# One half bank for all three terms of a product, pairs of column tiles per bank, fewer convolution taps on GpSimd

## The chip, the cores and the metric

One core of a Trainium2 chip runs the whole layer. The metric is device time in microseconds (us) of one launch, lower is better. The engines are named as in the profile: PE is TensorE's matmul side, PEld its weight load, DVE is VectorE, ACT is ScalarE, POOL is GpSimd, SP is SyncE, which issues the transfers.

## The reference, cut to what matters

One layer on 256 tokens with 2048 channels (16 row tiles of 128), everything in float32:

```
h = RMSNorm(x);  u = h @ W_in                       # 34 column tiles of 128
A: 6 heads   y_A = B * conv3(C * v)                 # short heads, 3 tiles each
B: 6 heads   GLU -> causal conv of 31 taps -> LayerNorm -> swish   # 2 tiles each
C: 4 groups  trailing mean over 2, 4, 8, 16 frames minus self -> 128x128 product
x = x + RMSNorm(concat(y_A, y_B, y_C) @ W_out)      # 16 column tiles
h = RMSNorm(x);  [g, v] = conv3(h @ W_up)           # 88 column tiles
x = x + RMSNorm((silu(g) * v) @ W_down)             # 44 row tiles
```

The scale of RMSNorm is one number for each token, so the kernel multiplies by it after the product (`r_bc`: the scales spread over all partitions), not before.

## The kernel before, in words

**The stream.** The weights come as 364 units of half a megabyte, [128 x 1024] float32: 68 of w_in, 32 of w_out, 176 of w_up, 88 of w_down, numbered through, so w_out begins at unit 68 and w_up at unit 100. Each unit is split into two float32r parts: ACT copies it to `whi` (L101), DVE subtracts that from the raw unit and leaves `wlo` (L108). `ahead(i)` splits up to unit i + 4. Two units of w_up (`POOL_UNITS`, 105 and 107) are subtracted by POOL. A unit holds 8 blocks of 128x128, for 8 products.

**The product** (L231 to L245). Activations lie as (hi, lo) pairs, 2 x 256 columns. For one block and one row tile PE runs a 512-column matmul `w_hi @ [h_hi, h_lo]` (L243) and a 256-column one, `w_lo @ h_hi` (L233); a column tile has a bank of its own. The bank's halves are added up afterwards: `fold` (L273) copies the right half with ACT (L275) and adds it with DVE (L276). Only the last tile of w_out, o15, uses the form `folded`: three 256-column matmuls into one half (L236, L237, L233).

**The order.** The first 4 column tiles of w_in, w_out and w_up are computed together (`mm_group`, 2 row tiles for each unit, 8 units), since their operands come only little by little; all others one after the other (`mm_columns`, 2 units, 16 products). `IN_ORDER`: the conformer heads' pairs (value, gate), the 4 pools, then the short heads. After each column tile some steps of `background` are issued (`PACE`). Small products (pool, LayerNorm's mean) are issued by `later` a number of units after their operand. A scheduler that estimates times puts the unpinned instructions of every engine in an order at build time; at run time each engine works in that order and only waits.

**A conformer head.** `head_glu` folds value and gate, scales them, and multiplies them on POOL (`glu`). Of its 31 taps, DVE takes 15 as multiply-adds (`tap`, L372); for the other `POOL_TAPS` = 14 ACT makes the scaled copies (L391) and POOL adds them up (L392). After the sixth head LayerNorm follows: POOL adds the heads up (`lnt`, L419), PE sums that over the channels (`ln_mean`, L425), and so on.

**Second norm and gated MLP.** The scale of the first norm comes back as `bc_y`; DVE scales y (L615), adds x (L619) and makes h's low part (L299), ACT its high part, two row tiles for each unit of the first group of w_up. A gate pair j (`gate`) folds both its tiles, scales them by `r2_bc` (L690), makes the two three-tap convolutions (ACT L691, DVE L693), Silu (ACT L700), product (POOL L702) and the two parts (ACT L703, DVE L704). At j = 4 and some later pairs DVE also transposes a part of the residual (L671). Row tiles 0 and 1 of the group wait for `r2_bc`, which is made after the group.

Of the kernel before, what the change touches and what calls it, by code (L numbers as in the profile page):

```python
# [14 lines left out]
P = 128  # L15
T = 256
# [10 lines left out]
# Columns of the packed per-channel parameters.  # L27
# [6 lines left out]
for _name, _w in _FIELDS:  # L34
# [9 lines left out]
IN_ORDER = (  # L44
    [x for i in range(N_HEADS) for x in (18 + i, 24 + i)]
    + [30 + g for g in range(N_POOL)]
    + [x for i in range(N_HEADS) for x in (6 + i, 12 + i, i)]
)
# The order in which the row tiles of w_out are contracted.
# [13 lines left out]
def trunk_kernel(ctx: ExitStack, tc, xt, vec, g_row, pool_w, w_in, w_out, w_up, w_down, out):  # L63
# [39 lines left out]
    def split_lo(i, pieces=1):  # L103
        raw = raws.pop(i)
        hi, lo = parts[i]
        eng = nc.gpsimd if i in POOL_UNITS else nc.vector
        for s in cut(pieces):
            ins = eng.tensor_tensor(lo[:, s], raw[:, s], hi[:, s].bitcast(F32), ALU.subtract)  # L108
            if eng is nc.vector:
                pin(ins)  # L110
# [15 lines left out]

# [1 line left out]
    # `background` holds elementwise work in order; `late` holds small products that  # L128
    # are issued a few units after their operands were, so that TensorE needn't wait.
# [41 lines left out]
    # TensorE's clock rises while it works: it is kept busy until the first weights are in.  # L171
    # The first activation loads ScalarE's table in that time.
    idle = const.tile([P, 512], BF16, name="idle")
# [4 lines left out]
    def keep_busy(n):  # L178
        warm = psum.tile([P, 512], F32, tag="mm", name="warm")
        for _ in range(n):  # L180
            tc.keep_in_program_order(
                nc.tensor.matmul(warm, idle[:, :P], idle, start=True, stop=True)
            )
# [20 lines left out]
    def squares_by_token(parts_, name):  # L204
        """Tiles [channels, n * T] that add up to the squares -> [tokens, 2 halves], in PSUM."""
# [13 lines left out]
    def over_partitions(r, name):  # L219
        """[tokens, 2 halves] -> [all partitions, tokens], in PSUM."""  # L220
# [8 lines left out]
    # Activations are kept as [channels, k, (hi, lo), T]; a product leaves w_hi @ lo in the  # L229
    # second half of its bank, or adds it to the first where `folded` is set.  # L230
    def product(ps, w_hi, w_lo, h, first, last, folded=False):  # L231
        def by_lo():
            nc.tensor.matmul(ps[:, :T], w_lo, h[:, 0], start=False, stop=folded and last)  # L233

        if folded:
            nc.tensor.matmul(ps[:, :T], w_hi, h[:, 0], start=first, stop=False)  # L236
            nc.tensor.matmul(ps[:, :T], w_hi, h[:, 1], start=False, stop=False)  # L237
            by_lo()
            return
        if last:  # L240
            by_lo()
        both = h.rearrange("p j t -> p (j t)")
        nc.tensor.matmul(ps, w_hi, both, start=first, stop=last)  # L243
        if not last:
            by_lo()  # L245

    def mm_columns(u0, name, ht, order=NATURAL, folded=False):
        ps = psum.tile([P, 512], F32, tag="mm", name=name)
        for h in range(2):
            ahead(u0 + h)  # L250
            whi, wlo = parts.pop(u0 + h)
            for kk in range(8):
                k = 8 * h + kk
                c = slice(kk * P, (kk + 1) * P)
                product(ps, whi[:, c], wlo[:, c], ht[:, order[k]], k == 0, k == KD - 1, folded)
            tick()
        return ps

    def mm_group(u0, name, ht, before, order=NATURAL):
        pss = [psum.tile([P, 512], F32, tag="mm", name=f"{name}{m}") for m in range(GROUP)]  # L260
        for kg in range(8):
            before(kg)
            ahead(u0 + kg)
            whi, wlo = parts.pop(u0 + kg)
            for kk in range(2):
                k = 2 * kg + kk
                for m, ps in enumerate(pss):
                    c = slice((kk * GROUP + m) * P, (kk * GROUP + m + 1) * P)
                    product(ps, whi[:, c], wlo[:, c], ht[:, order[k]], k == 0, k == KD - 1)
            tick()  # L270
        return pss

    def fold(ps, right, out):  # L273
        """The two halves of a bank, added up; `right` is scratch."""
        nc.scalar.activation(right, ps[:, T:], AF.Copy)  # L275
        nc.vector.tensor_tensor(out, ps[:, :T], right, ALU.add)  # L276
        return out

    # ================= token mixing =================
    with tc.tile_pool(name="mix", bufs=1) as mix, tc.tile_pool(name="mixt", bufs=2) as mixt:  # L280
# [23 lines left out]
        def start(kg):  # L304
            for k in (2 * kg, 2 * kg + 1):
                make_hi(k, h1, "g_mix")
                make_lo(k, h1, "g_mix")
                if k == 0:
                    split_hi(0, 2)
                    split_lo(0, 2)  # L310
                    done[0] = 1
            if 0 < kg < 5:
                load_x(2 * kg + 6, 2)
            square_sum(two(xT, kg), sum_x, kg == 0, f"sqx{kg}")

        first = mm_group(0, "in", h1, start)
        got = dict(zip(IN_ORDER, first))

# [28 lines left out]
        def tmp(name):  # L347
            return mixt.tile([P, T], F32, tag="t", bufs=10, name=name)

        def folded(ps, name):  # L350
            return fold(ps, tmp(f"{name}r"), tmp(name))
# [494 lines left out]
```

## Time and profile before

| | us |
|---|---|
| median of 3 runs | 1096.47 (1096.30 to 1096.82) |
| span of the profiled execution | 1094.2 |
| PE busy | 1050.7 (96%) |
| DVE busy | 774.7 (71%) |
| ACT busy | 593.6 (54%) |
| POOL busy | 244.9 (22%) |
| granted TensorE clock, mean over the span | 0.993 |

The span runs from the first to the last instruction of one execution; the time of a run is some 2.3 us longer. Busy time is not time on the path: PE is at work nearly all the time, so what can be won or lost is the time in which PE waits or runs at a lower clock, and the number and length of its matmuls. The chain that ended last is mostly PE's own; where it leaves PE, it leaves it for what PE waited for. A start in the timeline and the next start of the same kind give the pitch, which is what a pipelined matmul costs; its printed length (its end is modelled) is longer than that.

### The profile page before, as it was taken

The numbers are of one execution on the slowest core, as the hardware profiler recorded it, in microseconds if no ns is written. First come the engines' busy times: TensorE is split into PE (matmuls) and PEld (weight loads), VectorE is DVE, ScalarE is ACT, GpSimd is POOL, SyncE is SP. The second block draws the span as 40 slices with busy tenths as digits, with TensorE's granted clock in tenths as the row PEclk, the third lists the DMA queues.
The fourth block names the chain that finished last, engine by engine and source line by source line (L and its number), as shares of the span: only waits on it lengthen the run. The fifth ranks groups of instructions, "written<-read, shape, count | busy, mean of one in ns | idle before, by whom it ended". The sixth has DMA issues, their size and how long they took to land.

```text
span 1094.2 us, 15331 instructions
## 1 busy us (share of the span) xinstructions
PE 1050.7 (96%) x5565; PEld 885.7 (81%) x5565; DVE 774.7 (71%) x1042; ACT 593.6 (54%) x920; POOL 244.9 (22%) x260
## 2 busy tenths in 40 slices
PE   8987989699998999999999999999999999999997
PEld 5876778588886888888888888888888888888885
DVE  7899986775549886877778788788787444444444
ACT  8674466565555655655556566555555343343432
POOL 4386479742224220101101010000000000000001
PEclk9999999899999999999999999999999999999999
DMA  7634554446553537666486676555556655565552
GB/s 270 214 128 142 177 173 147 158 158 208 183 186 113 174 122 244 187 169 226 138 246 190 175 234 207 179 190 189 185 183 228 192 182 188 191 191 183 187 189 77
DMA packets 73452, 199.78 MB, mean 183 GB/s; under 512 B 23712, under 2 KB 24480, under 8 KB 73248
## 3 DMA queue, kind: packets, MB, share of 16 engines
q1 hardware_dynamic: 73088, 197.72, 56.9%
q8 instruction: 44, 0.72, 0.3%
q10 hardware_dynamic: 288, 1.07, 0.2%
q14 instruction: 32, 0.26, 0.1%
HBM read 194.57 MB, written 2.10 MB: 180 GB/s over the span
## 4 chain that ended last, share of the span: by engine, by line
PE 82%; DVE 7%; POOL 6%; issue 3%; ACT 1%; DMA 0%; SPq 0%; DVEq 0%; POOLq 0%; ACTq 0%
PE gate L243 14%; PE val L243 14%; PE d L736 8%; PE d L737 8%; PE d L738 7%; PE gate L233 7%; PE val L233 7%; PE o L243 5%; PE in L243 4%; POOL accp L392 3%; PE o L233 3%; DVE acc L372 3%; PE in L233 2%; DVE wlo L108 2%; DVE h L299 1%
## 5 line engine op out<-in xcount | busy, mean ns | idle before, releaser
L108 DVE TENSOR_TENSOR wlo<-raw,whi 128x1024 fp32r<-128x1024 f32 (+1 forms) x363 | 465.3, 1286 | 225.7 <-ACT whi L101 223.1
L101 ACT ACTIVATE whi<-raw 128x1024 fp32r<-128x1024 f32 (+1 forms) x365 | 383.1, 1053 | 264.8 <-PE d L738 135.1
L243 PE MATMUL gate<-h,whi 128*128 128x512 f32 x672 | 241.1, 399 | 0.0
L243 PE MATMUL val<-h,whi 128*128 128x512 f32 x672 | 241.0, 399 | 0.0
L243 PE MATMUL in<-h,whi 128*128 128x512 f32 x544 | 193.2, 403 | 4.2 <-DVE h L299 2.7
L233 PE MATMUL gate<-h,wlo 128*128 128x256 f32 x672 | 182.1, 281 | 0.0
L233 PE MATMUL val<-h,wlo 128*128 128x256 f32 x672 | 182.0, 281 | 0.0
L233 PE MATMUL in<-h,wlo 128*128 128x256 f32 x544 | 149.1, 287 | 12.2 <-DVE wlo L108 12.2
L243 PEld LDWEIGHTS val<-h,whi 128*128 128x128 f32 x672 | 126.4, 188 | 27.1
L243 PEld LDWEIGHTS gate<-h,whi 128*128 128x128 f32 x672 | 126.4, 188 | 26.9
L702 POOL TENSOR_TENSOR cg<-cg,cv 128x256 f32<-128x256 f32 x44 | 49.2, 1118 | 426.1 <-DVE cv L693 386.9
L738 PE MATMUL d<-whi,g_lo 128*128 128x512 f32 x352 | 138.8, 394 | 0.0
L736 PE MATMUL d<-whi,g_hi 128*128 128x512 f32 x352 | 138.8, 394 | 0.0
L737 PE MATMUL d<-wlo,g_hi 128*128 128x512 f32 x352 | 138.8, 394 | 0.0
L233 PEld LDWEIGHTS gate<-h,wlo 128*128 128x128 f32 x672 | 127.0, 189 | 4.9 <-DVE wlo L108 0.7
L233 PEld LDWEIGHTS val<-h,wlo 128*128 128x128 f32 x672 | 127.0, 189 | 4.2
L243 PEld LDWEIGHTS in<-h,whi 128*128 128x128 f32 x544 | 101.7, 191 | 26.9 <-DVE h L299 3.6
L233 PEld LDWEIGHTS in<-h,wlo 128*128 128x128 f32 x544 | 103.1, 191 | 21.1 <-DVE wlo L108 18.5
L243 PE MATMUL o<-y_t,whi 128*128 128x512 f32 x240 | 83.7, 395 | 0.0
L736 PEld LDWEIGHTS d<-whi,g_hi 128*128 128x128 f32 x352 | 65.9, 187 | 16.4
L738 PEld LDWEIGHTS d<-whi,g_lo 128*128 128x128 f32 x352 | 65.9, 187 | 16.2
L737 PEld LDWEIGHTS d<-wlo,g_hi 128*128 128x128 f32 x352 | 65.9, 187 | 16.2
(232 smaller groups left out, 1066.3 us busy)
## 6 DMA issues: line engine op xcount, KB each, us to landing
raw<-in_w_up SPq DMA_DIRECT2D x176, 512.0 KB, 3.7
raw<-in_w_down SPq DMA_DIRECT2D x88, 512.0 KB, 3.5
raw<-in_w_in SPq DMA_DIRECT2D x67, 512.0 KB, 3.8
raw<-in_w_out SPq DMA_DIRECT2D x32, 512.0 KB, 3.5
xT<-blocks SPq DMA_DIRECT2D x64, 32.0 KB, 3.8
out<-tail_sb SPq DMA_DIRECT2D x8, 256.0 KB, 2.3
xT<-in_xt SPq DMA_DIRECT2D x7, 256.0 KB, 5.5
tail_sb<-in_g_row ACTq DMA_DIRECT2D x1, 1024.0 KB, 6.7
```

The lines of the kernel that those rows point to most:

```text
L101: pin(nc.scalar.activation(hi[:, s], raws[i][:, s], AF.Copy))
L108: ins = eng.tensor_tensor(lo[:, s], raw[:, s], hi[:, s].bitcast(F32), ALU.subtract)
L233: nc.tensor.matmul(ps[:, :T], w_lo, h[:, 0], start=False, stop=folded and last)
L243: nc.tensor.matmul(ps, w_hi, both, start=first, stop=last)
L299: pin(nc.vector.scalar_tensor_tensor(ht[:, k, 1], xT[:, k], v(gain, k), ht[:, k, 0].bitcast(F32), ALU.mult, ALU.subtract,))
L372: nc.vector.scalar_tensor_tensor(a[:, o:], glu[:, : T - o], cb(s), a[:, o:], ALU.mult, ALU.add)
L392: nc.gpsimd.tensor_tensor(ap[:, o:], ap[:, o:], p[:, : T - o], ALU.add)
L702: nc.gpsimd.tensor_tensor(a, a, b, ALU.mult)
L736: nc.tensor.matmul(pss[h], g_hi[:, k, s], w1, start=(k == 0), stop=False)
L737: nc.tensor.matmul(pss[h], g_hi[:, k, s], w2, start=False, stop=False)
L738: nc.tensor.matmul(pss[h], g_lo[:, k, s], w1, start=False, stop=(k == KF - 1))
```

## The change

`product` now always makes three 256-column matmuls into one half bank, w_hi with h_hi, w_hi with h_lo, w_lo with h_hi, so nothing is folded. Two column tiles share a bank, one in each half (`mm_column`, `mm_pair`), and are read out together where they belong together: one 512-wide DVE multiply by the scale for a conformer head (`vg`), a gate pair (`u`) or two short heads' B tiles (`br`); the squares and copies of w_out's tiles read PSUM on ACT without a fold. The scalings of the short heads' C and B tiles and of the heads' values, on POOL before, are on DVE now. `POOL_TAPS` is 8, so DVE takes 21 taps of a head and POOL adds 7 copies and the sum. `POOL_UNITS` is gone. The first group of w_out and of w_up holds 8 column tiles (one row tile for each unit, 16 units), that of w_in still 4. Short heads come two at a time (C and v, C and v, B and B). `tmp` has 7 buffers instead of 10. The background's steps are counted by kind of pair (`PACE`) and in w_out 4 for each unit until the tenth. In the second norm the steps are spread over units of one row tile.

```diff
-GROUP = 4
+GROUP_IN, GROUP_OUT, GROUP_UP = 4, 8, 8
-POOL_UNITS = (68 + 32 + 5, 68 + 32 + 7)
-POOL_TAPS = 14  # taps of a conformer head that GpSimd adds up
+POOL_TAPS = 8
-PACE = (5, 4, 4)
+PACE = {"head": 5, "pool": 4, "cv": 4, "b": 5}
...
+    def product(ps, w_hi, w_lo, h, first, last):
+        terms = ((w_hi, h[:, 0]), (w_hi, h[:, 1]), (w_lo, h[:, 0]))
+        for n, (w, x) in enumerate(terms):
+            nc.tensor.matmul(
+                ps, w, x, start=first and n == 0, stop=last and n == 2, skip_group_check=True
+            )
...
+    def mm_pair(u0, name, ht, order=NATURAL, between=None):
+        ps = bank(name)
+        mm_column(u0, ps[:, 0], ht, True, order)
+        if between:
+            between()
+        mm_column(u0 + 2, ps[:, 1], ht, False, order)
         return ps
...
-        def head_glu(i, val, gate):
-            sg = folded(gate, f"sg{i}")
-            nc.vector.tensor_tensor(sg, sg, stats["r"], ALU.mult)
-            nc.scalar.activation(sg, sg, AF.Sigmoid)
-            vr = folded(val, f"vr{i}")
-            nc.gpsimd.tensor_tensor(vr, vr, stats["r"], ALU.mult)
+        def head_glu(i, ps):
+            vg = mixt.tile([P, 2, T], F32, tag="vg", name=f"vg{i}")
+            nc.vector.tensor_tensor(vg, ps, twice(stats["r"]), ALU.mult)
+            nc.scalar.activation(vg[:, 1], vg[:, 1], AF.Sigmoid)
             glu = glu6[:, i]
-            nc.gpsimd.tensor_tensor(glu, vr, sg, ALU.mult)
+            nc.gpsimd.tensor_tensor(glu, vg[:, 0], vg[:, 1], ALU.mult)
...
-        def gate(j, pg, pv):
-            a = conv3(pg, j, "cg")
+        def gate(j, ps):
+            u = ffnt.tile([P, 2, T], F32, tag="u", name=f"u{j}")
+            nc.vector.tensor_tensor(u, ps, twice(r2_bc), ALU.mult)
+            a = conv3(u[:, 0], j, "cg")
             nc.scalar.activation(a, a, AF.Silu)
-            b = conv3(pv, KF + j, "cv")
+            b = conv3(u[:, 1], KF + j, "cv")
...
-        for j in range(GROUP // 2, KF):
-            pg = mm_columns(u0, f"gate{j}", h2)
-            if j == GROUP // 2:
-                for i in range(j):
-                    gate(i, *first[2 * i : 2 * i + 2])
-            pv = mm_columns(u0 + 2, f"val{j}", h2)
+        n_first = GROUP_UP // 2
+        for j in range(n_first, KF):
+            ps = mm_pair(
+                u0, f"gv{j}", h2,
+                between=(lambda: [gate(i, first[i]) for i in range(n_first)])
+                if j == n_first else None,
+            )
             u0 += 4
-            gate(j, pg, pv)
+            gate(j, ps)
```

How this moves instructions is shown at two places. The first is DVE where the gated MLP has just begun. Before, the single tile gate5 (`gate_4012`) is folded and scaled between the transpose and the split of units 124 and 125 (`wlo_4016` and the next), before which PE still has val5's two units (122, 123) to do:

```order
L671 STREAM_TRANSPOSE blocks_4010<-xT 128x1024
L276 TENSOR_TENSOR u_4102<-gate_4012,cg_4103 128x256
L690 TENSOR_TENSOR u_4102<-u_4102,r_bc 128x256
L693 SCALAR_TENSOR_TENSOR cg_4103<-u_4102,vec_sb,cg_4103 128x255
L693 SCALAR_TENSOR_TENSOR cg_4103<-u_4102,vec_sb,cg_4103 128x254
L108 TENSOR_TENSOR wlo_4016<-raw_4013,whi_4015 128x1024
L108 TENSOR_TENSOR wlo_4038<-raw_4035,whi_4037 128x1024
```

Now the pair gv5 (`gv_4614`, units 120 to 123) stands there, and `wlo_4618` is unit 124, the first of the next pair; the split before it on DVE, unit 123's, lies 30 rows ahead:

```order
L710 TENSOR_TENSOR u_4735<-gv_4614,r_bc 128x512
L703 SCALAR_TENSOR_TENSOR cg_4737<-u_4735,vec_sb,cg_4737 128x255
L703 SCALAR_TENSOR_TENSOR cv_4742<-u_4735,vec_sb,cv_4742 128x255
L703 SCALAR_TENSOR_TENSOR cg_4737<-u_4735,vec_sb,cg_4737 128x254
L716 TENSOR_TENSOR g_lo<-cg_4600,g_hi 128x256
L684 STREAM_TRANSPOSE blocks_4612<-xT 128x1024
L703 SCALAR_TENSOR_TENSOR cv_4742<-u_4735,vec_sb,cv_4742 128x254
L114 TENSOR_TENSOR wlo_4618<-raw_4615,whi_4617 128x1024
```

What moved is the read of a finished tile: it now stands ahead of the split of the unit that PE takes right after that tile. On ACT at the same place the row of before is this, with the copy of the unit (`whi_4015`) one step behind gate5's convolution:

```order
L703 ACTIVATE g_hi<-cg_3991 128x256
L275 ACTIVATE cg_4103<-gate_4012 128x256
L691 ACTIVATE cg_4103<-u_4102,vec_sb 128x256
L101 ACTIVATE whi_4015<-raw_4013 128x1024
L101 ACTIVATE whi_4037<-raw_4035 128x1024
L700 ACTIVATE cg_4103<-cg_4103 128x256
```

Now both convolutions of gv5 and its Silu stand ahead of unit 124's copy (`whi_4617`):

```order
L701 ACTIVATE cg_4737<-u_4735,vec_sb 128x256
L701 ACTIVATE cv_4742<-u_4735,vec_sb 128x256
L715 ACTIVATE g_hi<-cg_4600 128x256
L712 ACTIVATE cg_4737<-cg_4737 128x256
L108 ACTIVATE whi_4617<-raw_4615 128x1024
```

Unit 124's copy has moved behind work that needs the last product of unit 123. The second place is POOL ahead of LayerNorm's mean, at the end of w_in before (the sum `lnt_994` is what `ln_mean` reads, and the short heads' scalings `br` and `cr` stand between):

```order
L392 TENSOR_TENSOR accp<-accp,p_30_1984 128x243
L521 TENSOR_TENSOR br_2099<-br_2099,r_bc 128x256
L395 TENSOR_TENSOR acc_408<-acc_408,accp 128x240
L523 TENSOR_TENSOR ya_2103<-br_2099,sa_2040 128x256
L377 TENSOR_TENSOR acc_408<-acc_408 128x255
L419 TENSOR_TENSOR lnt_994<-lnt_994,acc_408 128x256
L507 TENSOR_TENSOR cr_2164<-cr_2164,rr_bc 128x256
```

Now those scalings are gone from POOL, the sum is `lnt_1089`, and PE's `ln_mean` stands among the products of the w_out group, after the second of its 16 units:

```order
L399 TENSOR_TENSOR accp<-accp,p_30_2523 128x249
L402 TENSOR_TENSOR acc_470<-acc_470,accp 128x234
L384 TENSOR_TENSOR acc_470<-acc_470 128x255
L426 TENSOR_TENSOR lnt_1089<-lnt_1089,acc_470 128x256
L526 TENSOR_TENSOR br_2726<-br_2726,sa_2437 128x256
```

## Rows read from the trace of the kernel before

**Rows 1.** The page: span, and the chain that ended last by engine.

```profile
span 1094.2 us, 15331 instructions
...
PE 82%; DVE 7%; POOL 6%; issue 3%; ACT 1%; DMA 0%; SPq 0%; DVEq 0%; POOLq 0%; ACTq 0%
```

**Rows 2.** Waits of PE, 36 to 240 us: total us, times, longest.

```profile
PE in L233 <- DVE wlo L108: 11.9, 13, 2.2
PE ln_mean L425 <- POOL lnt L419: 7.5, 1, 7.5
PE pool L493 <- DVE pooled L486: 5.3, 4, 1.7
```

**Rows 3.** PE's timeline, start and length: first product after the group, first of w_out.

```profile
36.58 0.47 PE L243 MATMUL in<-h,whi 128*128 128x512 f32 x1
...
239.55 0.40 PE L243 MATMUL o<-y_t,whi 128*128 128x512 f32 x1
```

**Rows 4.** Windows: length, busy PE, PEld, DVE, ACT, POOL, PE clock, DMA, GB/s.

```profile
197.00:207.00 10.00, 5.19 (x26) 3.54 (x24) 8.72 (x11) 6.30 (x11) 9.53 (x11) 1.00 0.34 116
207.00:217.00 10.00, 5.08 (x19) 4.34 (x20) 7.21 (x11) 4.27 (x9) 6.22 (x8) 0.66 0.54 169
```

**Rows 5.** DVE's timeline in w_in: splits of units 16 and 43, taps, a quiet split.

```profile
53.06 1.22 DVE L108 TENSOR_TENSOR wlo<-raw,whi 128x1024 fp32r<-128x1024 f32 x1
...
74.77 3.43 DVE L372 SCALAR_TENSOR_TENSOR acc<-glu,vec_sb,acc 128x252 f32<-128x252 f32 x4
...
126.12 1.22 DVE L108 TENSOR_TENSOR wlo<-raw,whi 128x1024 fp32r<-128x1024 f32 x1
127.26 1.23 DVE L372 SCALAR_TENSOR_TENSOR acc<-glu,vec_sb,acc 128x250 f32<-128x250 f32 x3
...
144.83 1.22 DVE L108 TENSOR_TENSOR wlo<-raw,whi 128x1024 fp32r<-128x1024 f32 x1
```

**Rows 6.** POOL's timeline beside the first taps of rows 5.

```profile
77.02 8.12 POOL L392 TENSOR_TENSOR accp<-accp,p 128x251 f32<-128x251 f32 x8
```

**Rows 7.** PE's timeline: products of o14, of o15 (folded form), two tiles of w_up.

```profile
318.72 0.39 PE L243 MATMUL o<-y_t,whi 128*128 128x512 f32 x1
...
323.25 0.40 PE L243 MATMUL o<-y_t,whi 128*128 128x512 f32 x1
...
324.31 0.28 PE L236 MATMUL o<-y_t,whi 128*128 128x256 f32 x1
...
328.20 0.28 PE L236 MATMUL o<-y_t,whi 128*128 128x256 f32 x1
...
828.17 0.40 PE L243 MATMUL gate<-h,whi 128*128 128x512 f32 x1
...
833.82 0.40 PE L243 MATMUL val<-h,whi 128*128 128x512 f32 x1
```

**Rows 8.** Waits of PE over the whole span, the first group of w_up.

```profile
PE up L243 <- DVE h L299: 4.6, 4, 2.1
```

**Rows 9.** Timelines of DVE and POOL in that group.

```profile
349.00 4.03 DVE L299 SCALAR_TENSOR_TENSOR h<-xT,vec_sb,h 128x256 fp32r<-128x256 f32 x2
...
350.18 2.56 POOL L108 TENSOR_TENSOR wlo<-raw,whi 128x1024 fp32r<-128x1024 f32 x1
```

**Rows 10.** Timelines of DVE and ACT: durations used for the gate pairs.

```profile
335.73 0.68 DVE L615 TENSOR_TENSOR yo<-yo,bc_y 128x512 f32<-128x512 f32 x1
...
396.47 0.48 DVE L693 SCALAR_TENSOR_TENSOR cv<-u,vec_sb,cv 128x254 f32<-128x254 f32 x1
...
404.45 1.24 DVE L671 STREAM_TRANSPOSE blocks<-xT 128x1024 f32<-128x1024 f32 x1
...
406.55 0.60 ACT L691 ACTIVATE cg<-u,vec_sb 128x256 f32<-128x256 f32 x1 [1.67 <-DVE u L690]
407.06 1.99 ACT L101 ACTIVATE whi<-raw 128x1024 fp32r<-128x1024 f32 x2
408.95 0.40 ACT L700 ACTIVATE cg<-cg 128x256 f32<-128x256 f32 x1
```

More of the change, by code (lines that the diff above doesn't have):

```diff
@@ L227, in over_partitions, with bank, mm_column @@
         return ps[:, :T]
[L231 to L248, printed above, removed]
+    def product(ps, w_hi, w_lo, h, first, last):
+        terms = ((w_hi, h[:, 0]), (w_hi, h[:, 1]), (w_lo, h[:, 0]))
+        for n, (w, x) in enumerate(terms):
+            nc.tensor.matmul(
+                ps, w, x, start=first and n == 0, stop=last and n == 2, skip_group_check=True
+            )
+    def bank(name):
+        return psum.tile([P, 2, T], F32, tag="mm", name=name)
+    def mm_column(u0, ps, ht, opens, order=NATURAL):
         for h in range(2):
@@ L254, in mm_columns, with mm_group, twice @@
                 c = slice(kk * P, (kk + 1) * P)
-                product(ps, whi[:, c], wlo[:, c], ht[:, order[k]], k == 0, k == KD - 1, folded)
+                product(ps, whi[:, c], wlo[:, c], ht[:, order[k]], opens and k == 0, k == KD - 1)
             tick()
-        return ps
[L259 to L269, printed above, removed]
+    def mm_pair(u0, name, ht, order=NATURAL, between=None):
[4 more added lines that the diff above has]
+        mm_column(u0 + 2, ps[:, 1], ht, False, order)
+        return ps
+    def mm_group(u0, name, ht, n, before, order=NATURAL):
+        pss = [bank(f"{name}{m}") for m in range(n // 2)]
+        rows = 8 // n
+        for u in range(KD // rows):
+            for kk in range(rows):
+                before(rows * u + kk)
+            ahead(u0 + u)
+            whi, wlo = parts.pop(u0 + u)
+            for kk in range(rows):
+                k = rows * u + kk
+                for m in range(n):
+                    c = slice((kk * n + m) * P, (kk * n + m + 1) * P)
+                    product(
+                        pss[m // 2][:, m % 2], whi[:, c], wlo[:, c], ht[:, order[k]],
+                        k == 0 and m % 2 == 0, k == KD - 1,
+                    )
             tick()
         return pss
[L273 to L277, printed above, removed]
+    def twice(t):
+        return t[:, None, :].to_broadcast([P, 2, T])
     with tc.tile_pool(name="mix", bufs=1) as mix, tc.tile_pool(name="mixt", bufs=2) as mixt:
@@ L302, in make_lo, with start @@
             ))
[L304 to L317, printed above, removed]
+        def start(k):
+            make_hi(k, h1, "g_mix")
+            make_lo(k, h1, "g_mix")
+            if k == 0:
+                split_hi(0, 2)
+                split_lo(0, 2)
+                done[0] = 1
+            kg = k // 2
+            if k % 2:
+                if 0 < kg < 5:
+                    load_x(2 * kg + 6, 2)
+                square_sum(two(xT, kg), sum_x, kg == 0, f"sqx{kg}")
+        first = mm_group(0, "in", h1, GROUP_IN, start)
         edge = mix.tile([P, N_POOL, 16], F32, name="edge")
@@ new lines, in short_conv, with short_gate @@
+            nc.vector.tensor_tensor(cv, ps[:, 1], cv, ALU.mult)
+            a = tmp(f"sa{i}")
+            nc.scalar.activation(a, cv, AF.Copy, scale=ca(2))
+            for s in (1, 2):
+                nc.vector.scalar_tensor_tensor(
+                    a[:, s:], cv[:, : T - s], ca(2 - s), a[:, s:], ALU.mult, ALU.add
+                )
+            stats[f"a{i}"] = a
+        def short_gate(i, ps):
+            br = mixt.tile([P, 2, T], F32, tag="vg", name=f"br{i}")
+            nc.vector.tensor_tensor(br, ps, twice(stats["r"]), ALU.mult)
+            for j in range(2):
+                nc.gpsimd.tensor_tensor(br[:, j], br[:, j], stats.pop(f"a{i + j}"), ALU.mult)
+                keep(i + j, br[:, j])
@@ L552, in trunk_kernel, with scales_a, between @@
+        def scales_a():
+            stats["rx"] = token_rsqrt([sum_x], D, RMS_EPS, "x")
+        later(1, scales_a)
+        later(2, token_scales)
+        def between(kind):
             while waiting:
                 evacuate(*waiting.pop(0))
-            run_background(PACE[0 if 18 <= m < 30 else 1 if m >= 30 else 2])
-        sum_y = mix.tile([P, T], F32, name="sum_y")
+            run_background(PACE[kind])
+        for kind, i, _ in IN_PAIRS[GROUP_IN // 2 :]:
+            ps = mm_pair(u0, f"in_{kind}{i}", h1, between=lambda: between(kind))
+            u0 += 4
+            waiting.append((kind, i, ps))
+            between(kind)
@@ L810, in _lay_out, with by_columns @@
     ], axis=1))
-    def by_columns(w, order, rows=None):
+    def by_columns(w, order, group, rows=None):
         t = w.reshape(KD, P, -1, P)
```

207 lines of the change are left out of this document (94 added, 113 removed).

## The prediction, made before the changed kernel ran

> **What bounds the kernel now.** I read the page first: the chain that ended last is 82% PE, with 7% DVE and 6% POOL, in a span of 1094.2 us; a run takes 1096.47, so 2.3 us lie outside the span and I add them at the end [rows 1]. The kernel is bound by PE's matmuls; the 13% of DVE and POOL are places where PE waited for them. So I asked next for PE's waits, and then for PE's timeline stage by stage, against the time that the products alone would take.
>
> The pitch of a product, start to start, is (833.82 − 828.17)/16 = 353.1 ns over a whole w_up tile [rows 7]. In w_in, from the first product after the group to the first of w_out, there are 59 units of 8 products: 472 x 0.3531 = 166.7 us, with the small products (scales, pools, LayerNorm) perhaps 5 more. It took 239.55 − 36.58 = 203.0 us [rows 3]. So **31 us are lost in w_in**: 11.9 in 13 waits for DVE's `wlo`, 5.3 in 4 waits of the pool products for DVE's `pooled`, 7.5 in one wait of `ln_mean` for POOL's `lnt` [rows 2]. The other 6 or so are slow matmuls: after the long wait the granted clock is 0.66 of 2.4 GHz in the mean of 207 to 217, part of the 10 us at the lower level, 1.2 GHz, worth up to 3.4 us [rows 4]; the rest lies around the shorter waits. The other place is the first group of w_up, with 4.6 us in 4 waits for h's low part [rows 8]. Everywhere else PE streams, and there only the product itself counts.
>
> **Why DVE is late in w_in.** Between the splits of units 16 and 43 it took 144.83 − 53.06 = 91.8 us, while PE needs 27 x 8 x 0.3531 = 76.3 [rows 5]. A tap costs (1.23 − 0.48)/2 = 0.38 quiet, start to start (three in 1.23, one alone being 0.48 long), and 3.43/4 = 0.86 or a little less while POOL adds [rows 5, 6, 10]. POOL's eight adds took 8.12, 1.0 each [rows 6], so each costs DVE some 0.46. Quiet, by the order of before: 27 splits x 1.14 + 80 taps x 0.38 + 22 others x 0.34 = 68.7; the missing 23.1 are some 50 POOL operations.
>
> **Part 1, w_in: −15.** The change takes away 34 folds on DVE and ACT and about 54 operations on POOL, and gives DVE 36 more taps and the multiplies that POOL had. By the order of after, the same 27 units hold 85 taps, 3 multiplies of 512 (0.60) and 15 others: 27 x 1.14 + 85 x 0.38 + 1.8 + 15 x 0.34 = 70.0 quiet. So in this stretch the taps eat what the folds give. What is left is a little less disturbance, about 46 POOL operations: 70.0 + 46 x 0.46 = 91.2, against 76.3 that PE needs: 15 us behind, less the lead of a unit or so with which the stretch begins, plus the pool products, which now come in two pairs right ahead of the splits of units 37 and 43 and so wait no further. I take 14 us of waits and 1 of slow clock, where before 17 of waits and 3 stand. The wait of `ln_mean` (7.5) and its slow clock (3.4) I take as gone: POOL was busy 9.53 of 10 us ahead of it [rows 4], now two thirds of that queue are left, and PE meets `ln_mean` at unit 70 instead of 59, 11 units of 2.8 us later. Behind unit 43 DVE has room (no wait of size for `wlo` stands there). So 31 − 15 − 1 for pieces = 15 gained. Bounds: −5 if POOL's operations disturb DVE as much as before and the taps come on top (36 x 0.38 = 13.7 less 34 folds x 0.34 = 11.6, spread unevenly), −25 if DVE's relief leaves waits of only 6.
>
> What those operations take from each other is a price of this trace, 0.46 us for 1.0 us of POOL. The Trainium skill (SBUF — State Buffer, Who interferes with whom) says that a DVE instruction with two SBUF inputs contends with a GpSimd one that reads, and that whichever comes second fully blocks. By that rule each POOL add that goes would give back up to its whole duration, twice what I take; the trace shows 0.46 of 1.0, so the sum doesn't use it; the first rival is what it would do here.
>
> **Part 2, first group of w_up: −5.5.** With 8 tiles a row tile gives PE 8 products, 2.83 us, and DVE's work for it is half a scaling and half an addition of 512 (0.68 together), one L299 (0.48) and one split (1.14), 2.3 us [rows 5, 10]. POOL no longer splits two units there, which made two of L299 last 4.03 [rows 9]. The 4.6 us of waits go [rows 8], and about 1 more: the first matmul of a product asks for h_hi alone, no longer for both parts (0.5), and the first matmul after each wait ran slower. Bounds −4.6 and −6.5.
>
> **Part 3, the product form: +4.** Both forms stand in rows 7: o14's inside a tile (323.25 − 318.72)/13 = 348.5 ns, o15's three matmuls (328.20 − 324.31)/11 = 353.6, w_up's 353.1 with the tile's edge. Per product +0.5 against w_up and +5.1 against o14; w_up is 1408 of the 2208 products (138 tiles x 16), so I take 1.8: 2208 x 1.8 = +4.0, between +1.1 and +11.3. The third weight load of a product hides, as it does in o15: 118 ns for each matmul and its own load. The folds that go (88 in w_up) were beside PE's work and give nothing there.
>
> The Trainium skill (TensorE: Matmul & The Clock Gate, Back-to-back issue gap) gives a warm matmul N/2.4 + 2.5 ns, so a third matmul for the same columns would cost 2.5 ns; that is 2208 x 2.5 = 5.5 us and a time 1.5 later than mine, an estimate from that page. The same passage says that in a stream spacing is set by load and matmul together.
>
> **Part 4, the beginning of the gated MLP: +8.5.** This is a new wait. On DVE the scaling `u` of pair gv5 stands ahead of the split of unit 124, and on ACT both convolutions and the Silu of gv5 stand ahead of its copy. gv5 ends with unit 123, and PE goes on with 124. From the end E of unit 123: 0.2 to be seen, u 0.68, ACT 0.60 and 0.60, DVE's taps 0.48 and 0.4, Silu 0.40, the copy 1.0: whi at E + 4.4; DVE meanwhile has a g_lo (0.4), a transpose (1.24) and a tap (0.48), then the split 1.22: wlo at E + 6.1 [rows 5, 10]. PE has two matmuls to do with whi, 0.24, so it waits 5.9 in all. Before, the same row of work read gate5, which was done two units (5.6 us) before PE came to unit 124, so nothing waited. To that I add lateness: r2_bc comes at about unit 118.5, and 30 operations, the four pairs of the group and gv4, stand between the splits of units 123 and 124 on DVE (5 scalings x 0.60 + some 20 taps x 0.39 + 4 g_lo and the transpose, 13.5 quiet, up to 16 with POOL's products), against 5.5 units x 2.83 = 15.5: 0 to 2, say 1.5. And a pause of such length costs clock, as the one of 7.5 did [rows 2, 4]: say 1. In sum +8.5; bounds +5 (ACT finds u at once, no lateness) and +12. Later pairs have three to five units between the read of a pair and the next split, so I cost them nothing.
>
> **Costed at nothing**: w_out's group and tiles (ACT reads PSUM once for each tile more simply; PE streams, and LayerNorm's `finish` has until unit 78, where the conformer rows are contracted), the second norm's chain at the end of w_out (same steps), w_down and the tail (untouched). If LayerNorm were late, PE would wait at unit 78: cover 8 units, 22 us.
>
> **Sum**: −15 − 5.5 + 4 + 8.5 = −8. The execution's 1094.2 − 8 = 1086.2, and with 2.3 outside **1088.5**.
>
> **The rivals.**
> *A, DVE relieved more than I think.* POOL has some 50 fewer of 158 operations from the start to LayerNorm's squares. If a third of them goes in this stretch too, and each costs DVE its whole 1.0 us while it runs, 23.1/3 = 8 us come back instead of 2, and the waits in w_in are 8 instead of 14, with 1 less of slow clock; and if gv5's stall stays at its lower end, 5 instead of 8.5: 1088.5 − 7 − 3.5 = 1078. For it: rows 5 and 6 side by side. Against: the taps come to DVE in just the stretch in which it was 15 us behind. 0.19.
> *B, the taps keep DVE the bound.* 85 taps plus multiplies with disturbance as before, pools and units late, the gain of part 1 only 5: 1088.5 + 10 = 1098.5, no change to be seen. For it: quiet work of 68.7 against 70.0 is no relief. Against: the wait for POOL alone is 7.5 + 3.4. 0.13.
> *C, slower: the product's pitch.* Three matmuls in a row now add to the same half bank over all 2208 products, and a pair shares a bank that is read while the next fills. If the pitch were 362 ns instead of 354.9, that is +9 on 353.1: 2208 x 9 = +20 instead of +4, 1104.5. It decides from 2.2 us above the old time: without part 3 the sum is −12, so from 14.2/2208 = 6.4 ns for each product, 359.5 in all. For it: o15 is the only tile so made, 16 products. Against: that tile, with 353.6. 0.09.
> *D, the change doesn't do what it says*: the wait that goes in w_in comes back in the group of w_out, where `ln_mean` now stands, because POOL's `lnt` still lags; 7.5 + 3 of part 1 lost: 1099. 0.04.
>
> **How the numbers follow.** My case 0.55 (1083 to 1094), A 0.19 (1078), B 0.13, C 0.09, D 0.04. Low 1076.5 takes in A; high 1099 takes in B and most of D and leaves out C and a bit of A's far side. A measurement of this kernel can tell 0.2%, 2.2 us: faster is below 1094.3, slower above 1098.7. Faster: 0.55 + 0.19 and a part of B, 0.77; same: most of B, a part of D and the edge of mine, 0.12; slower: C and the rest, 0.11.
>
> **What would show it.** In the trace after: no wait of PE for `lnt`; waits for `wlo` and `pooled` in w_in of about 14 and w_out beginning near 224; in the first group of w_up no wait above 0.5; one stall of 6 to 9 us at unit 124 with DVE's split as its releaser; a product pitch of 353 to 356 ns in w_up. I'm wrong if the pitch is above 357, if w_out begins later than 232, or if unit 124 comes without a wait.

## The result, and the profile after

The changed kernel takes **1084.82 us** (median, 1084.73 to 1084.90) against 1096.64 for the kernel before in the same runs; the ratio is 0.9894, 95% interval 0.9880 to 0.9908. It is 11.8 us faster; 8 were forecast, 1088.5, and the result lies in the stated range. The sum was near by luck: the gain in w_in was taken some 12 us too small, and the loss by the product's pitch some 9 us too small.

The page of the changed kernel: span, busy time and the chain that ended last (what answers to [rows 1]).

```profile
span 1083.0 us, 19157 instructions
...
PE 1062.3 (98%) x7761; PEld 1007.5 (93%) x7761; DVE 708.5 (65%) x908; ACT 538.0 (50%) x740; POOL 192.4 (18%) x197
...
PE 91%; DVE 6%; issue 1%; ACT 1%; DMA 1%; SPq 0%; DVEq 0%; POOL 0%; ACTq 0%
```

POOL's 6% of the chain are gone and PE has 91% of it. PE's waits over the whole span, which answer to [rows 2] and [rows 8]:

```profile
PE gv L242 <- ACT whi L108: 4.3, 1, 4.3
PE in_head L242 <- DVE wlo L114: 2.0, 1, 2.0
PE pool L499 <- DVE pooled L492: 1.1, 1, 1.1
PE gv L242 <- DVE wlo L114: 1.0, 1, 1.0
```

Of the 24.7 us of waits in w_in 3.3 are left (the third and second row, and 0.2 for one more split). The wait for `lnt` is gone, that of the first w_up group too. New are 4.3 and 1.0 at one place of the gated MLP. To see where the time went I cut both executions at the same products. PE's timeline of the changed kernel: the first product after w_in's group, the first of w_out, of w_up and of w_down.

```profile
35.58 0.48 PE L242 MATMUL in_head<-h,whi 128*128 128x256 f32 x2
...
213.59 0.40 PE L242 MATMUL o<-y_t,whi 128*128 128x256 f32 x2
...
310.76 0.91 PE L242 MATMUL up<-h,whi 128*128 128x256 f32 x5
...
827.62 0.40 PE L749 MATMUL d<-whi,g_hi 128*128 128x512 f32 x1
```

and of the kernel before, where the first two cuts stand in [rows 3], the other two:

```profile
335.20 0.50 PE L243 MATMUL up<-h,whi 128*128 128x512 f32 x1 [0.43 <-DVE h L299]
...
839.47 0.40 PE L736 MATMUL d<-whi,g_hi 128*128 128x512 f32 x1
```

| stage | before | after | difference |
|---|---|---|---|
| start and group of w_in | 36.6 | 35.6 | -1.0 |
| rest of w_in | 203.0 | 178.0 | -25.0 |
| w_out and second norm | 95.6 | 97.2 | +1.5 |
| w_up, gated MLP | 504.3 | 516.9 | +12.6 |
| w_down to the end of the span | 254.7 | 255.4 | +0.7 |

So the change won 26 us up to w_out and gave more than half of it back behind that (14.8). Most of the 1.5 in w_out is moved and not lost: LayerNorm's small products (`ln_mean`, `ss_ln`, `bc_ln`, ten matmuls) ran in w_in before and run in w_out now, 1.7 us of busy time, so as much of the 25.0 isn't won. `ln_mean` before and after:

```profile
211.92 1.22 PE L425 MATMUL ln_mean<-lnt,ones 128*128 128x256 f32 x2 [7.51 <-POOL lnt L419]
```

```profile
219.25 0.59 PE L432 MATMUL ln_mean<-lnt,ones 128*128 128x256 f32 x2
```

The loss in w_up comes mostly from the pitch. Two w_lo matmuls of one stretch stand 13 products apart in each pair of rows here, first in the gated MLP, then in w_out (both of the changed kernel):

```profile
500.26 0.28 PE L242 MATMUL gv<-h,wlo 128*128 128x256 f32 x1
...
504.94 0.28 PE L242 MATMUL gv<-h,wlo 128*128 128x256 f32 x1
...
250.14 0.28 PE L242 MATMUL o<-y_t,wlo 128*128 128x256 f32 x1
...
254.73 0.28 PE L242 MATMUL o<-y_t,wlo 128*128 128x256 f32 x1
```

That is 4.68/13 = 360.0 ns for a product, 120.0 for each matmul, in the gated MLP, and 4.59/13 = 353.1 ns, 117.7, in w_out. Outside of the short stretches at a lower clock, all the matmuls that read h (w_in and w_up, 122 tiles) ran at 120.0, those that read y_t (w_out) at 117.7.

### The profile page after: what moved, and what is told of

Same layout as the page of the kernel before. It is cut to its first block, busy times and chain, and to the rows that moved or that the text cites. A ratio compares the mean times of both kernels' runs of the same rounds, so it can differ in the third digit from the quotient of the medians.

```text
span 1083.0 us, 19157 instructions
## 1 busy us (share of the span) xinstructions
PE 1062.3 (98%) x7761; PEld 1007.5 (93%) x7761; DVE 708.5 (65%) x908; ACT 538.0 (50%) x740; POOL 192.4 (18%) x197
## 3 DMA queue, kind: packets, MB, share of 16 engines
q10 hardware_dynamic: 288, 1.07, 0.3%
## 4 chain that ended last, share of the span: by engine, by line
PE 91%; DVE 6%; issue 1%; ACT 1%; DMA 1%; SPq 0%; DVEq 0%; POOL 0%; ACTq 0%
PE gv L242 43%; PE o L242 8%; PE d L751 8%; PE d L749 8%; PE d L750 8%; PE in_cv L242 6%; PE up L242 4%; DVE acc L379 3%; PE in_b L242 3%; PE in L242 2%; DVE wlo L114 1%; PE in_head L242 1%; DMA raw<-in_w_in 0%; DMA xT<-in_xt 0%; PE warm L188 0%
## 5 line engine op out<-in xcount | busy, mean ns | idle before, releaser
L242 PE MATMUL gv<-h,whi 128*128 128x256 f32 x2560 | 463.7, 284 | 4.3 <-ACT whi L108 4.3
L242 PEld LDWEIGHTS gv<-h,whi 128*128 128x128 f32 x2560 | 401.5, 193 | 4.5 <-ACT whi L108 4.5
L242 PE MATMUL gv<-h,wlo 128*128 128x256 f32 x1280 | 363.6, 284 | 1.0 <-DVE wlo L114 1.0
L242 PEld LDWEIGHTS gv<-h,wlo 128*128 128x128 f32 x1280 | 247.1, 193 | 1.2 <-DVE wlo L114 1.2
L242 PE MATMUL o<-y_t,whi 128*128 128x256 f32 x512 | 91.0, 280 | 0.0
L242 PEld LDWEIGHTS o<-y_t,whi 128*128 128x128 f32 x512 | 78.2, 188 | 0.1
L242 PE MATMUL o<-y_t,wlo 128*128 128x256 f32 x256 | 71.5, 279 | 0.0
L242 PE MATMUL in_cv<-h,whi 128*128 128x256 f32 x384 | 69.8, 284 | 0.0
L379 DVE SCALAR_TENSOR_TENSOR acc<-glu,vec_sb,acc 128x246 f32<-128x246 f32 (+10 forms) x126 | 66.6, 569 | 2.5 <-POOL acc L402 2.2
L242 PEld LDWEIGHTS in_cv<-h,whi 128*128 128x128 f32 x384 | 60.0, 192 | 0.1
```

The source lines that it names most:

```text
L242: nc.tensor.matmul(ps, w, x, start=first and n == 0, stop=last and n == 2, skip_group_check=True)
L379: nc.vector.scalar_tensor_tensor(a[:, o:], glu[:, : T - o], cb(s), a[:, o:], ALU.mult, ALU.add)
```

## The experiments

In each comparison the kernel before ran beside it; its medians were 1096.35 to 1096.71.

### e3: the taps back on GpSimd

```diff
-POOL_TAPS = 8
+POOL_TAPS = 14
```

> The changed kernel with 14 taps of a head on GpSimd again instead of 8, all else as changed. Theory 1, what relieved w_in is that POOL disturbs DVE less: in the stretch from the split of unit 16 to that of unit 43 some 18 more POOL adds and 18 fewer DVE taps, quiet work 70.0 - 6.9 = 63.1 and (27 + 18) x 0.46 = 20.7 of disturbance, 83.8 us instead of 78.8; PE's waits in w_in rise from 3 to 8 us or more, time 1090 to 1094. Theory 2, the folds and the scalings that went are what relieved it and the taps are nearly neutral: 1084 to 1086. Theory 3, DVE's own work counts most, so fewer taps on it help: below 1083.

Measured: 1103.57 us, ratio 1.0061 (1.0045 to 1.0078), **18.8 us more** than the changed kernel and 7 more than the kernel before. Theory 1 in kind, but it gave 5 to 9 us. All of it lies in w_in: from the first product after the group to the first of w_out it takes 196.6 us (36.31 to 232.90), 18.6 more than the changed kernel, and w_up keeps its pitch. All else of the change, without the six taps, is a loss (the pitch and the wait at unit 124 among it). The splits of units 16 and 43 in e3:

```profile
58.45 1.65 DVE L114 TENSOR_TENSOR wlo<-raw,whi 128x1024 fp32r<-128x1024 f32 x1
...
147.85 1.21 DVE L114 TENSOR_TENSOR wlo<-raw,whi 128x1024 fp32r<-128x1024 f32 x1
```

That is 89.4 us where 83.8 were expected, with 57 POOL operations beside it where 45 were expected. The same 90 us, 57 to 147, of the kernel before, the changed kernel and e3, in this order (windows: length, busy PE, PEld, DVE, ACT, POOL with counts, PE clock, DMA share, GB/s):

```profile
57.00:147.00 90.00, 77.17 (x413) 64.06 (x413) 90.00 (x126) 50.66 (x87) 55.15 (x57) 0.98 0.48 152
```

```profile
57.00:147.00 90.00, 86.99 (x700) 86.17 (x701) 90.00 (x151) 40.17 (x56) 31.86 (x32) 0.98 0.54 177
```

```profile
57.00:147.00 90.00, 76.73 (x577) 74.19 (x576) 90.00 (x121) 46.10 (x75) 56.95 (x61) 0.94 0.47 149
```

DVE is busy all 90 us in each, but it does 126, 151 and 121 instructions in that time, as POOL does 57, 32 and 61. Since DVE has no idle time there, fewer instructions mean longer ones: over the whole run the mean tap is 569 ns in the changed kernel and 704 in e3 (rows of L379 in the pages). The taps cost DVE less than what POOL's part of them took from it. PE's waits in e3:

```profile
PE in_head L242 <- DVE wlo L114: 6.1, 4, 2.8
PE pool L499 <- DVE pooled L492: 5.3, 3, 3.1
PE ln_mean L432 <- POOL lnt L426: 2.6, 1, 2.6
PE in_pool L242 <- DVE wlo L114: 1.6, 1, 1.6
```

The wait for POOL's `lnt` is back as well (2.6), though `ln_mean` stands in w_out there too. So its place by itself was not the cover that I took it for; POOL's shorter queue was part of it.

### e1, e2: h, the units and y_t moved together

The clean step of the pitch between h and y_t asked for a reason. First suspect: where the moving operand starts.

```diff
+        pad = const.tile([P, 16], F32, name="pad")
+        nc.vector.memset(pad, 0.0)
         h1 = const.tile([P, KD, 2, T], F32R, tag="ht", name="h1")
```

> The changed kernel with an unused 64-byte tile allocated ahead of h1, so that h1 and h2 start at byte 36832 of each partition instead of 36768, and everything allocated behind them (units, y_t) lies 64 bytes further too. In the changed kernel's trace a matmul that reads h has a pitch of 120.0 ns, one that reads y_t 117.8, from the first product of w_out on and back at the first of w_up. Theory 1, the place of the moving operand alone decides (h at 32 past a multiple of 128, y_t at 96): the two swap, h products at 117.8 (122 tiles x 48 matmuls x 2.2 ns = 12.9 us less), y_t products at 120.0 (16 x 48 x 2.2 = 1.7 us more), about 1073.6 us. Theory 2, the stage or the distance between operand and weights decides (both shift alike): pitch and time stay, 1084.8.

Measured: 1085.04 us, ratio 0.9895 (0.9880 to 0.9909). In the trace h products are at 360.0 and y_t products at 353.1 as before, theory 2.

> The same with a tile of 32 bytes: h starts at a multiple of 64 that is 64 past a multiple of 128, y_t at a multiple of 128. Theory 1 (place of the moving operand): both pitches change against the changed kernel; if what counts is starting at a multiple of 64, both come to 117.8 or below, 1072 us or less. Theory 2 (stage, or distance): 120.0 and 117.8 stay, 1084.8.

(8 instead of 16 in the diff.) Measured: 1085.25 us, ratio 0.9899 (0.9884 to 0.9913), the same pitches. The start of the operand by itself is out; a distance between operands, which neither run changed, is not.

### e6: w_out's products from h1

```diff
-        pss = mm_group(u0, "o", y_t, GROUP_OUT, mixing, OUT_ORDER)
+        pss = mm_group(u0, "o", h1, GROUP_OUT, mixing, OUT_ORDER)
```

(and the same in the other three calls of w_out)

> The changed kernel with w_out's products taking h1 as their moving operand instead of y_t (so the mixing's result isn't used in what follows). Theory 1, the operand (its place or its contents) makes the difference between 117.8 and 120.0 ns: w_out's matmuls come to 120.0, the span 768 x 2.2 ns = 1.7 us longer. Theory 2, the stage does (the weights, what the other engines do beside it): they stay at 117.8.

Measured: 1087.21 us in a single run, 2.4 more than the changed kernel; the evidence here is the pitch and not this time. The same stretch of w_out as above:

```profile
250.30 0.28 PE L242 MATMUL o<-h,wlo 128*128 128x256 f32 x1
...
254.98 0.28 PE L242 MATMUL o<-h,wlo 128*128 128x256 f32 x1
```

4.68/13 = 360.0 ns: w_out takes the pace of h. Theory 1: it is the operand, not the stage.

### e5: the weights moved away from h

```diff
         h1 = const.tile([P, KD, 2, T], F32R, tag="ht", name="h1")
+        pad = const.tile([P, 80], F32, name="pad")
+        nc.vector.memset(pad, 0.0)
```

> The changed kernel with an unused 320-byte tile allocated behind h1, so that h stays where it is and the units (whi, wlo) and y_t lie 320 bytes further. The distance from h to the first whi buffer was 51200 bytes, a multiple of 1024; that from whi to y_t stays 45888. Theory 1, the distance between the moving operand and the weights sets the pitch: the h products come down from 120.0 to 117.8 ns a matmul, 122 tiles x 48 x 2.2 ns = 12.9 us, to 1072. Theory 2, something else about the operand or the stage: 120.0 and 1084.8 stay.

Measured: 1057.1, 1057.5, 1072.8 and 1072.8 us in four executions; the ratio of all is 0.9712 (0.9637 to 0.9787). Theory 1, and more than it promised. In the profiled execution (1057.1) the h products run at two paces. In this order: the gated MLP at 500 us; the end of w_up's group and the start of the gated MLP, up to the eight small `ss_x` products at 357.96; the gated MLP behind them, at 362; and w_out.

```profile
500.30 0.28 PE L242 MATMUL gv<-h,wlo 128*128 128x256 f32 x1
...
504.72 0.28 PE L242 MATMUL gv<-h,wlo 128*128 128x256 f32 x1
...
353.09 0.28 PE L242 MATMUL up<-h,wlo 128*128 128x256 f32 x1
...
357.51 0.28 PE L242 MATMUL gv<-h,wlo 128*128 128x256 f32 x1
...
357.96 0.95 PE L218 MATMUL ss_x<-ones,sum 128*128 128x1 f32 x8
...
362.71 0.28 PE L242 MATMUL gv<-h,wlo 128*128 128x256 f32 x1
...
366.95 0.28 PE L242 MATMUL gv<-h,wlo 128*128 128x256 f32 x1
...
250.20 0.28 PE L242 MATMUL o<-y_t,wlo 128*128 128x256 f32 x1
...
254.79 0.28 PE L242 MATMUL o<-y_t,wlo 128*128 128x256 f32 x1
```

340.0 ns (4.42/13, 113.3 for a matmul) at 500 and, the same, from 353 to 357; 353.3 (4.24/12, 117.8) at 362; y_t's products unchanged at 353.1, with the weights moved but, by the addresses of the build, their distance to y_t not. In this trace the pace changes where the even stream of products is broken, and holds in between: broken by small products without any wait of PE (113.3 to 117.8 at `ss_x`), or by a pause (back to 113.3 behind the wait of 4.3 us at unit 124). What picks one of the two isn't shown. Of the two executions at 1072.8 there is no trace; 117.8 all through would make 1084.8 - 12.9 = 1071.9.

### e9, e10: two more distances, on the kernel with late gates (e7)

The diff is e5's with 64 and 96 for 80, on top of e7's (below: each gate pair is read half a pair later; 1077.27 us).

> The run with late gates (1077.3 us) with an unused 256-byte tile behind h1: the distance from h to whi is 51456 bytes, 256 past a multiple of 512 (0 in the changed kernel, pitch 120.0; 320 with the 320-byte tile, 113.3 or 117.8 from stage to stage; 192 from y_t, 117.8). Theory 1, the distance within 512 bytes sets the pitch of the h products: it isn't 120.0; between 113.3 and 117.8 the time is 1077.3 - 12.9 to 1077.3 - 39 = 1038 to 1064. Theory 2, only distances off a multiple of 64 bytes x odd or the like help and 256 falls on the same place as 0: 120.0 stays, 1077.

Measured: 1076.85 us, ratio 0.9821 (0.9806 to 0.9835), that of e7. Theory 2, for this distance.

> The same with 384 bytes. Theory 1: pitch of the h products between 113.3 and 117.8, 1038 to 1064, by how it compares with 256 the best place is bracketed. Theory 2 (every multiple of 128 is alike): 120.0, 1077.

Measured: 1071.81 us, ratio 0.9773 (0.9758 to 0.9787), 5.5 less than e7 by the medians. Pitch in the gated MLP of e9 and of e10, 12 products apart in both:

```profile
500.36 0.28 PE L242 MATMUL gv<-h,wlo 128*128 128x256 f32 x1
...
504.68 0.28 PE L242 MATMUL gv<-h,wlo 128*128 128x256 f32 x1
```

```profile
500.42 0.28 PE L242 MATMUL gv<-h,wlo 128*128 128x256 f32 x1
...
504.70 0.28 PE L242 MATMUL gv<-h,wlo 128*128 128x256 f32 x1
```

360.0 and 356.7 ns. For e10 neither theory holds as put: the pitch is below 120.0 but above 117.8. By the bytes put between h and the weights: 0 and 256 give 120.0 for a matmul, 384 gives 118.9, 320 gives 117.8 or 113.3. That the distance without them is a multiple of 512 comes from the build's addresses, which no trace holds. More points weren't run, and why it is so stays open.

### e11: the kernel before with the same tile

> The kernel before with the 320-byte tile behind h1, nothing else. Its products are one matmul of 512 and one of 256 columns. Theory 1, the distance acts on each matmul beside a weight load, and the 256-column one was at 120.0 there too (353.5 for a product, less 233.4 for 512 columns): a product comes down to 353.5 - 2.2 or 353.5 - 6.7, 1952 of them, 4 to 13 us less outside of what hides in waits, 1084 to 1093. Theory 2, the three-matmul form alone is sensitive to it: 1096.5. If the product comes down by more, the 512-column matmul gains too.

Measured: 1096.40 us, ratio 0.9998 (0.9989 to 1.0008). Theory 2. Its gated MLP, 11 products apart:

```profile
501.05 0.28 PE L233 MATMUL gate<-h,wlo 128*128 128x256 f32 x1
...
504.94 0.28 PE L233 MATMUL gate<-h,wlo 128*128 128x256 f32 x1
```

353.6 ns, what it was without. The form with one 512-column and one 256-column matmul took the same at both distances tried; the form with three of 256 goes from 360.0 down to 340.0. So the new form is the slower one by 6.4 ns a product where the change put it, and the faster one by 13.6 with the 320 bytes, at the faster of its two paces.

### e4, e7, e8: the wait at unit 124

The place, in the changed kernel: PE, then DVE and ACT, in their timelines.

```profile
385.84 0.50 PE L242 MATMUL gv<-h,whi 128*128 128x256 f32 x2 [4.34 <-ACT whi L108]
387.38 0.58 PE L242 MATMUL gv<-h,wlo 128*128 128x256 f32 x1 [1.03 <-DVE wlo L114]
...
381.54 0.69 DVE L710 TENSOR_TENSOR u<-gv,r_bc 128x512 f32<-128x512 f32 x1 [0.90 <-PE gv L242]
...
386.10 1.22 DVE L114 TENSOR_TENSOR wlo<-raw,whi 128x1024 fp32r<-128x1024 f32 x1
...
384.75 1.04 ACT L108 ACTIVATE whi<-raw 128x1024 fp32r<-128x1024 f32 x1
```

DVE takes up gv5 at 381.54, 0.2 us behind its last product, the copy starts at 384.75 and the split at 386.10: the chain of the prediction, step by step. Then PE's matmuls are slow up to 393.4. The window (columns as in e3):

```profile
390.00:400.00 10.00, 10.00 (x73) 10.00 (x73) 4.61 (x5) 3.43 (x4) 0.00 (x0) 0.83 0.86 239
```

73 matmuls stand in these 10 us, where e7 below has 86. The mean granted clock is 0.83, so for a third of the window it was at the lower of its two levels, 1.2 GHz; PE had just waited 4.34 and 1.03 us.

e4 read the first four pairs two at a time and kept splits and scalings in program order:

```diff
-            nc.vector.tensor_tensor(u, ps, twice(r2_bc), ALU.mult)
+            pin(nc.vector.tensor_tensor(u, ps, twice(r2_bc), ALU.mult))
...
+        late_of = {4: (0, 1), 5: (2, 3)}
         for j in range(n_first, KF):
+            pinned[0] = j < 8
...
```

> The changed kernel with the four gate pairs of the first group read out two at a time (0 and 1 between the columns of pair 4, 2 and 3 between those of pair 5), and, for pairs 4 to 7, the splits and the scaling of each pair kept in program order, so that no pair is read ahead of the split of the unit that PE takes next. Theory 1, the wait at unit 124 is made by that order alone: its 5.4 us and the slow matmuls behind it (about 3 us) go, 1076 to 1077. Theory 2, DVE has too much to do there in any order: the wait moves to a later unit, 1082 to 1085.

Measured: 1090.89 us, ratio 0.9947 (0.9930 to 0.9964), **6 us slower** than the changed kernel. Neither theory: PE's waits in the gated MLP are 7.5 us in all (5.0 for ACT's copy, 2.5 for DVE's split) instead of 5.4. DVE's timeline in e4 shows why:

```profile
371.45 0.43 DVE L716 TENSOR_TENSOR g_lo<-cg,g_hi 128x256 fp32r<-128x256 f32 x1 [1.47 <-ACT g_hi L715]
...
373.15 0.48 DVE L703 SCALAR_TENSOR_TENSOR cg<-u,vec_sb,cg 128x255 f32<-128x255 f32 x1 [0.67 <-ACT cg L701]
```

Kept in order, one gate follows the other with nothing between: DVE waits 1.47 for the round over ACT and POOL and 0.67 for ACT in each, 2 of 5 us, and the splits behind come late.

e7 reads each pair half a pair later, with nothing kept in order:

```diff
+        todo = [(i, first[i]) for i in range(n_first)]
+
+        def some(n):
+            for _ in range(min(n, len(todo))):
+                gate(*todo.pop(0))
...
+            ps = mm_pair(u0, f"gv{j}", h2, between=lambda: some(2))
...
-            gate(j, ps)
+            todo.append((j, ps))
...
+        some(2)
```

> The changed kernel with each gate pair read out half a pair later, between the columns of the next pair (the four of the first group two at a time), with nothing kept in program order; by the order the splits and the gate work now alternate on DVE and ACT, and no split stands behind a read of the unit just before it. Theory 1, order alone made the wait at unit 124 (and the run before, kept in program order, made each gate serial): no wait of PE at the start of the gated MLP, 5.4 us and about 3 of slow clock less, 1076 to 1077. Theory 2, DVE or ACT has too much to do there whatever the order: a wait of 3 us or more stays, 1081 or more.

Measured: 1077.27 us, ratio 0.9824 (0.9807 to 0.9840), 7.5 less than the changed kernel, theory 1; PE has no wait there, and its matmuls keep their pace (86 from 380 to 390, and in the next window):

```profile
390.00:400.00 10.00, 10.00 (x86) 10.00 (x85) 9.55 (x17) 7.32 (x12) 1.99 (x3) 1.00 0.79 251
```

e8 leaves the reads as they are and moves the transposes:

```diff
-            if 4 <= j < 28:
-                c, at = divmod(j - 4, 6)
+            if 10 <= j < 34:
+                c, at = divmod(j - 10, 6)
```

> The changed kernel with the four transposes of the residual at pairs 10, 16, 22 and 28 instead of 4, 10, 16 and 22, nothing else changed. By the order unit 124's splits then no longer stand behind the read of pair gv5. Theory 1, the transpose's buffer, which is one of the four raw units, is what pushed unit 124 behind gv5, and the burst of the first gates by itself fits: no wait, 1076 to 1077. Theory 2, the burst of the first gates is what counts: the wait stays within 2 us of what it was, 1083 to 1085.

Measured: 1077.29 us, ratio 0.9823 (0.9809 to 0.9838), the same 7.5, theory 1. In its trace DVE splits a unit between the first gates again, and unit 124 stands ahead of gv5, so the burst of 30 operations by itself costs nothing. That it is the transpose's buffer which pushed the split back is argued: by the kernel it takes one of the four raw buffers just while the first gates are read, and from 380 to 390 the DMA engines were busy 0.09 of the time in the changed kernel and 0.61 in e8. No run moved DVE's 1.24 us alone and kept the buffer.

### e12: late gates and 320 bytes together

> The late gates and the 320-byte tile behind h1 together. Theory 1, the two gains add up and the distance of 320 past a multiple of 512 lets the h products run at one of two paces, 113.3 or 117.8 ns, chosen anew after each pause of PE: with 117.8 all through the gated MLP 1077.3 - 12.9 = 1064, with 113.3 all through 1077.3 - 39 = 1038, and executions of the same program differ by some 10 us or more, as 1057 and 1073 did. Theory 2, the pause at the start of the gated MLP is what brought 113.3, and without it the slower pace stays: 1064 in every execution.

Measured: 1046.8, 1049.5, 1065.8, 1065.9, 1066.0 and 1067.2 us, median 1065.87, against 1096.35 before. The profiled execution is the one of 1046.8, and its gated MLP runs at 113.3 from within pair 4 on, behind the small `bc_x` products, without a pause of PE. So theory 2, that it takes the pause, is out. Of those at 1066 there is no trace; 117.8 in place of 113.3 in the 80 tiles of w_up behind the group would be 80 x 48 x 4.5 ns = 17.3 us, close to the 16 to 20 that lie between the two groups of times. Theory 1 fits; that the slower four ran at 117.8 is not shown. The worst of these executions is still 18 us below the changed kernel. The best that is steady is e10, 1071.8.

## Why the prediction was right, and where it was not

**What bounds the kernel** was right: PE's waits in w_in, one group of w_up, and the product.

**Part 1** was too small, by a count. Forecast: 15 us gained, waits of 14 left. Measured: 25.0 in the stage, in which the pitch cost 472 x 6.5 ns = 3.1; less LayerNorm's small products, which only moved, some 27 gained, and waits of 3.3 left; w_out began at 213.6 where 224 was forecast. The step that failed is "about 46 POOL operations" in the stretch from unit 16 to unit 43. There were 27, as against 55 before (the prediction's "some 50"). DVE's splits of units 16 and 43 in the changed kernel:

```profile
56.96 1.65 DVE L114 TENSOR_TENSOR wlo<-raw,whi 128x1024 fp32r<-128x1024 f32 x1
...
135.81 1.21 DVE L114 TENSOR_TENSOR wlo<-raw,whi 128x1024 fp32r<-128x1024 f32 x1
```

78.9 us, against 91.8 before [rows 5] and 91.2 forecast. The quiet work, 70.0, was right, and so was roughly the price: 70.0 + 27 x 0.46 = 82.4; by these rows the price is (78.9 - 70.0)/27 = 0.33 us for a POOL operation of 1.07, and before 23.1/55 = 0.42. I had set POOL's row of the order beside DVE's as if they kept step. They don't: with fewer taps POOL runs out of work and waits. Of its 42 tap additions 13 began before this stretch and 21 behind it. Groups of POOL by line, idle time before them at the end: the additions in the stretch before, then three groups of the changed kernel in 57 to 136.

```profile
L392 POOL TENSOR_TENSOR accp<-accp,p 128x251 f32<-128x251 f32 (+12 forms) x35 | 33.2, 952 | 7.3 <-ACT p L391 5.8
```

```profile
L399 POOL TENSOR_TENSOR accp<-accp,p 128x250 f32<-128x250 f32 (+6 forms) x9 | 9.3, 1035 | 1.0 <-ACT p L398 0.4
...
L384 POOL TENSOR_TENSOR acc<-acc 128x255 f32<-128x255 f32 x2 | 4.0, 2012 | 12.6 <-DVE acc L379 12.6
...
L370 POOL TENSOR_TENSOR glu<-vg 128x256 f32<-128x256 f32 x3 | 2.9, 972 | 17.1 <-ACT vg L368 17.1
```

Rival A had the mechanism, and gave it 8 us where it was 13: it let a third of POOL's operations go from this stretch, and half of them went. The 1.0 us that it allowed for the price of one was not it. The Trainium skill calls the ports that DVE and GpSimd share an exclusive lock (SBUF — State Buffer, Who interferes with whom). In the mean these rows show DVE losing a third to two fifths of POOL's time, not all of it; what POOL loses to DVE wasn't worked out.

**Part 2** was right: no wait of PE in the first group of w_up.

**Part 3** was too small: +4 forecast, with +11.3 as the upper end. Measured: 360.0 in place of 353.1 [rows 7] to 353.6 (e11), some 6.5 ns on the 1952 products that read h, 12.7 us, and at most 0.5 in w_out. The prediction named a pitch above 357 as showing it wrong, and here it was. The step that failed is that o15's three matmuls [rows 7] stand for all: o15 reads y_t, and 1952 of 2208 products read h. Its 353.6 was right for w_out and for nothing else. What sets the pitch in its place is the moving operand together with where the weights lie (e5, e6). Rival C named the mechanism's price (362 ns, and the tile that was the only one of its kind) but not its reason; at +13 instead of +20 and with part 1's larger gain the result stayed on the faster side.

**Part 4** was right in place, chain and size: 5.4 us of waits and about 2 more of slow matmuls, 7.5 by e7 and e8, against 8.5 (the stall alone is a little below the 6 to 9 us named, and ACT's copy ended most of it). That the wait hangs on where the first transpose stands was not seen; the burst's lateness, for which 1.5 stood, costs nothing by itself (e8).

**Costed at nothing**: w_out and the norm cost 1.5, most of it LayerNorm's small products, moved there from w_in. The 0.7 from w_down on is open.

Rival B fell with the 3.3 us of waits left in w_in, and D with the wait for `lnt` gone; by e3 the relief comes with the taps.

## What to carry to other kernels

Price a new form of a matmul on the operand that it will read: the same instruction ran at 120.0 ns on one tile and 117.7 on another. Where two engines share work, count how many operations of one really fall into the stretch in which the other is late; an order says what follows what on one engine, not what runs beside it. A buffer that a side job borrows from the stream can put the stream's next unit behind a read that waits.

## What the runs showed of the hardware

The pitch of a 256-column matmul with a weight load of its own depends here on how far the weights lie behind the moving operand in SBUF: 120.0 ns as the change put them and with 256 bytes more, 118.9 with 384 more, 117.8 or 113.3 with 320 more (e5, e9, e10; e1 and e2 with the distance kept show no change). That only the remainder within 512 bytes counts wasn't tested: no run put 512 bytes in. With 320 the pace changes where the stream is broken, by a pause or by other small products, and is kept in between (traces of e5 and e12); the executions of one program lay 15 to 20 us apart there, and that the paces make this difference fits the sum but was not traced. The form of 512 and 256 columns stayed at 353.6 ns for a product without and with the 320 bytes (e11).
